# Weight chunks at three layer seams split later, GLA's sums moved to VectorE, and norms moved back in differential attention

## The chip, the cores and the metric

The kernel runs on one core of a Trainium2 chip. The metric is device time of one execution in microseconds (us), lower is better. Three runs of the kernel before took 1218.33, 1220.27 and 1220.82, median 1220.27. Engines are named as in the profile: PE is TensorE, DVE VectorE, ACT ScalarE, POOL GpSimd, and SP the queue that loads the weights.

## What is computed

An AdaLN block and then two more layers, on 256 tokens of width 1024, in fp32 (cut to what the change touches):

```python
# first block: SwiGLU, mixer (short convolution and S5 state space), SwiGLU, final norm
mod = silu(cond) @ w_mod + b_mod                # nine shift, scale and gate rows
x = x + 0.5 * g1 * swiglu(modulate(rms_norm(x, ffn1_norm), sh1, sc1), ffn1_w_gate, ffn1_w_up, ffn1_w_down)
x = x + g2 * mixer(modulate(rms_norm(x, mix_norm), sh2, sc2))
x = x + 0.5 * g3 * swiglu(modulate(rms_norm(x, ffn2_norm), sh3, sc3), ffn2_w_gate, ffn2_w_up, ffn2_w_down)
h = rms_norm(x, final_norm)
# layer 0: gated linear attention (GLA, 4 heads) and an MLP
q, k, v, g, z = split(rms_norm(h, a_norm) @ a_w_in)
log_a = log_sigmoid(z @ w_gate_up + b_gate) / 16          # b = cumsum(log_a) in chunks of 64 tokens
o = causal_sum(q_i . k_j * exp(b_i - b_j)) v_j            # by key, inside and across the chunks
h = h + (rms_norm(o, head_gain) * silu(g)) @ a_w_out
h = h + square(relu(rms_norm(h, mlp_norm0) @ mlp_w1_0)) @ mlp_w2_0
# layer 1: differential attention (8 heads, two maps each), and an MLP
k, v = split(rms_norm(h, kv_norm) @ w_kv); k = rms_norm(k); q = rms_norm(rms_norm(h, b_norm) @ w_q) / 8
a = softmax(q0 k0) - lam * softmax(q1 k1)
h = h + (rms_norm(a @ v, head_gain) * (1 - lambda_init)) @ b_w_out
h = h + square(relu(rms_norm(h, mlp_norm1) @ mlp_w1_1)) @ mlp_w2_1
```

## The kernel before

**Weights.** Each product is made in fp32 out of three matmuls: a weight chunk of 1 MB (128 x 2048) is loaded by SP (L156) into one of three `stage` buffers, ScalarE rounds it into `wh` (L185, two halves of 128x1024), VectorE subtracts to make `wl` (L187, two halves), and `mm3` (L262) runs `wh`, `wl` and `wh` once more against the high and low part of the other operand. `schedule()` writes the order of all chunks down. `Stream.prep` splits the next chunks as long as one of four (later five) slots is free, and `load` issues the load of chunk k once chunk k-3 has been split, since it takes over that buffer. `take(name, j, ahead)` first splits up to `ahead` chunks beyond the one it takes, without an argument as many as there are slots; with `ahead=0` nothing beyond it. A place in the order of `schedule()` decides what is loaded behind what; a place of `prep` in the program decides where the split stands in ScalarE's and VectorE's instructions. Each engine runs its instructions in program order.

**Seams.** `ffn()` (L485) runs a feed-forward layer in steps of 256 hidden units: the up (and gate) chunk of a step is taken and multiplied, the activation makes `hidf`, ScalarE and VectorE split it in `hidh` and `hidl`, and the down product of an earlier step runs beside it. The last three down chunks are taken at its end and go, with the products that use them, into a `Tail`. Down products sum to `acc[i][f]`, i the half of the tokens and f the half of the columns. `turn()` (L438) is the seam: the tail's parts for token half 0, `post(0)` (VectorE adds `acc` to the residual `x`, L398 and L399, ScalarE sums squares, L311), the first of the tail's parts for token half 1, a `prep`, `evac(0)` (the norm's root, then PE transposes into `xnT`, L349, split into `hTh` and `hTl`), the late parts, a `prep`, `post(1)`, and then the first chunks of the new layer on token half 0, with `evac(1)` after the second one. At the seam of ffn2 there is a norm more, the block's final one (L983 to L995). A `swap(n)` after a layer's chunks puts the last down chunk behind the first n chunks of the next layer.

**GLA** (L1284) multiplies the gate, then in `featb` the queries and keys feature by feature (a_in 0 to 3); the values and output gates are a_in 4 to 11. The gate's four products (L1336) become the log decay `E` (L1341 to L1345), a scan over the tokens makes `b`. Six levels of pairs (spans of 1 to 32 tokens) each need `level_e` (differences of `b`, two sums, L1363 and L1364), `exp`, `level_x` (four products with q and k, L1374 to L1378) and `level_mm` on PE (L1385). `across_e`, `across_x` and `across` do the pairs of different chunks (L1426 to L1440). The differences run on GpSimd (name `gt`).

**Differential attention** (L1607): `keys`, `queries` and `values` each take a chunk, multiply and (keys, queries) norm it by head with `qk_norm` (L1628 to L1634, root on ScalarE L303); `turn_qk` transposes, `scores` (L1698), the softmax (L1709 to L1721), `turn_a` (transposes `aT`, copied out by ScalarE, L1733), `outputs` (L1743 to L1752). Four groups of heads run staggered.

Of the kernel before, what the change touches and what calls it, by code (L numbers as in the profile page):

```python
# [18 lines left out]
S = 256  # L19
D = 1024  # L20
KD = 8
CW = 256
# [33 lines left out]
def schedule():  # L56
# [36 lines left out]
    def swap(n):  # L93

        behind.append((len(it) + n, it[-1]))
# [8 lines left out]
    ffn("ffn1", MODS_FFN1, 1)  # L104
    swap(2)
    md = [4 * g + c for g in MODS_MIXER for c in range(4)]
# [29 lines left out]
class Stream:  # L136
# [63 lines left out]
    def take(self, name, j=0, ahead=10 ** 9):  # L200
        self.n_take += 1
        self.prep(self.n_take + ahead)
        W, slot = self.ready.pop((name, j))
        self.used.append(slot)
        return W


class Net:
# [277 lines left out]
    def ffn(self, tail, evac, ups, dn, steps, gated, post, side=None, n_first=3):  # L486
# [48 lines left out]
        for s in range(n_first, steps):  # L535
            res = []
            for u in ups:
                ps = self.bank_u("up")
                begins = s == n_first and u == ups[0]
                self.feat(self.take(u, s, 0 if begins else 10 ** 9), self.hT, v3(ps, 2))  # L540
                self.S.free()
                if s == steps - 1 and u == ups[-1]:
                    self.S.locked.discard((dn, steps - 1))
                res.append(ps)
                if begins:
                    for b in range(n_first):
                        first_hid(b)
                    self.S.prep(10 ** 9)
                    acc = self.acc_banks()
# [12 lines left out]
            if side is not None:  # L562
                side(s)
        last = [(hd, self.take(dn, steps - 3 + n)) for n, hd in enumerate(pend)]
        if gated:
# [718 lines left out]
def gla(N, tail, evac, c):  # L1284
    nc, t, t2, take = N.nc, N.t, N.t2, N.take
    ones, misc, ident = c["ones"], c["misc"], N.ident
    vt, gt, act = nc.vector.tensor_tensor, nc.gpsimd.tensor_tensor, nc.scalar.activation
    v = [t([D], "macc", bufs=2) for i in range(2)]
# [26 lines left out]

    wz = [v3(w, KD) for w in take("a_z")]
    zp = N.bank_u("z")[:16, :S]
# [4 lines left out]

    def featb(ch, dst, scale):
        ps = N.bank_u("qk")
        N.feat(take("a_in", ch), N.hT, v3(ps, 2))
        N.S.free()
        act(out=flat(dst), in_=ps, func=AF.Copy, scale=scale)

    qT, kT = t2([4, S], "qT"), t2([4, S], "kT")
    featb(0, qT[:, 0:2, :], 128 ** -0.5)  # L1330
    gp = []
    for h2 in range(2):
        ps = N.bank_a("gate")
        for k in range(2):
            h = 2 * h2 + k
            nc.tensor.matmul(ps[:, S * k:S * k + S], wgu[:16, 128 * h:128 * h + 128], zT[:16, :], start=True, stop=True)  # L1336
        gp.append(ps)
    e1, mn = t2([4, S], "E", bufs=2), t2([4, S], "E", bufs=2)
# [17 lines left out]
    def level_e(li):  # L1356

        s = LEVELS[li]
        nb = 512 // s
        E = Es[li] = t2([4, S], "E", bufs=2)  # L1360
        ev, bv = (flat(z).rearrange("p (n two s) -> p n two s", two=2, s=s) for z in (E, b))
        ref = bv[:, :, 0, s - 1:s].to_broadcast([128, nb, s])
        gt(out=ev[:, :, 1, :], in0=bv[:, :, 1, :], in1=ref, op=SUB)  # L1363
        gt(out=ev[:, :, 0, :], in0=ref, in1=bv[:, :, 0, :], op=SUB)  # L1364

# [50 lines left out]
    def across_e():  # L1416
# [8 lines left out]
        for i in range(2):  # L1425
            gt(out=ec[:, :, 2 * i, :], in0=tot(2 * i), in1=bc[:, :, 2 * i, :], op=SUB)  # L1426
            nc.gpsimd.tensor_copy(out=ec[:, :, 2 * i + 1, :], in_=bc[:, :, 2 * i + 1, :])
        gt(out=e2[:, :, 0, :], in0=ec[:, :, 0, :], in1=tot(1), op=ADD)
        gt(out=e2[:, :, 1, :], in0=tot(1), in1=bc[:, :, 1, :], op=SUB)
        nc.gpsimd.tensor_copy(out=e2[:, :, 2, :], in_=bc[:, :, 2, :])  # L1430
        gt(out=e2[:, :, 3, :], in0=bc[:, :, 3, :], in1=tot(2), op=ADD)
        xa.extend((E, E2))
# [27 lines left out]
    featb(3, kT[:, 2:4, :], 1.0)  # L1460
    W = take("a_in", 7)
    vt(out=kss[:, 2], in0=qf, in1=kf, op=MUL)
    level_x(0)
    level_e(2)
    exp(Es[2])
    level_x(1)
    level_e(3)
# [10 lines left out]

    W = take("a_in", 8)
    level_x(2)  # L1480
    level_e(4)
    exp(Es[4])
    level_x(3)
    level_e(5)
# [3 lines left out]
    level_mm(3)  # L1488
    W = take("a_in", 9)
    level_x(4)  # L1490
    level_x(5)
    across_e()
    for E in xa:
        exp(E)
    gate_chunk(1, W)
    level_mm(4)
# [3 lines left out]
    gate_chunk(2)  # L1500
    across()
    for hd in range(3):
        act(out=sg[hd], in_=sg[hd], func=AF.Silu)
# [28 lines left out]
    for hp in range(2):  # L1532
        for i in range(2):
            av(i, hp)
    for hd in range(3):
        gated(hd)
    nc.scalar.preload_act_table(AF.Silu)
    W = take("a_in", 11)
    ps = N.bank_u("vg")
    for i in range(2):  # L1540
        N.tokm(W, N.hT, i, ps[:, CW * i:CW * i + CW])
    N.S.free()
    act(out=flat(sg[3]), in_=ps, func=AF.Silu)
    c["load"]("m0", t([D], "macc", bufs=2))
# [62 lines left out]
def diff(N, tail, c):  # L1607
# [171 lines left out]
    turn_qk(1)  # L1779
    queries(2)  # L1780
    turn_a(0)
    scores(1, N.bank_a)
    values(1)
    outputs(0)
    keys(3)
    turn_a(1)
    turn_qk(2)
    turn_o(0)
    queries(3)
    outputs(1)  # L1790
    scores(2, N.bank_a)
    values(2)
# [116 lines left out]
```

## Time and profile before

| what | value |
|---|---|
| median of three runs | 1220.27 us |
| profiled execution | 1219.3 us |
| its span (first to last instruction) | 1217.6 us |
| mean granted clock of TensorE | 0.959 of full |
| PE busy | 1135.3 us, 93% of the span |
| DVE busy | 793.7 us, 65% |
| ACT busy | 613.4 us, 50% |
| POOL busy | 236.6 us, 19% |

A busy share is a mean over stages with different limits. A timeline row gives the start, the length, the engine, the line, the output and the inputs, how many instructions it joins, and in brackets the idle time of the engine before it with the instruction that ended it. PEclk is TensorE's granted clock as a share of its full 2.4 GHz; 0.50 is its lower level of 1.2 GHz. A row `wh<-stage` is a cast of a weight chunk, `wl<-stage,wh` its subtraction. The places that the change touches are ffn1 to mixer (241 to 280 us), ffn2 to GLA (560 to 600), GLA (600 to 700), mlp0 to differential attention (875 to 902) and the attention (925 to 1021).

### The profile page before, as it was taken

To read this page: it belongs to the slowest core of one execution; us is meant where nothing else is said; L and a number is where in the kernel's file an instruction comes from. 1 tells how busy PE (TensorE), PEld (TensorE's weight loads), DVE (VectorE), ACT (ScalarE), POOL (GpSimd) and SP (SyncE) were. 2 spreads that over 40 slices of the span, in tenths; PEclk is the share of its full clock that TensorE was granted. 3 is DMA by queue.
4 is the path that set the end of the run, shared out by engine and by line. 5 is a ranking of instruction groups with operands and counts; after the bars stand their busy time and mean duration, and the time that the engine had idled before them with its cause. 6 is when DMAs were issued, how large, how long until landed. Compare 5 with 4: busy or idle time off the path is not lost.

```text
span 1217.6 us, 18757 instructions
## 1 busy us (share of the span) xinstructions
PE 1135.3 (93%) x7780; PEld 1051.7 (86%) x7780; DVE 793.7 (65%) x934; ACT 613.4 (50%) x941; POOL 236.6 (19%) x304
## 2 busy tenths in 40 slices
PE   1698999989789999999798999999999899999998
PEld 1697999979778999998798889999989897999997
DVE  7698797667968785565466665644468776564541
ACT  3444434455084554354364656655446764664541
POOL 8996399400500000000224100000000000000000
PEclk9698999989789999999897999999999899999999
DMA  8588787535243786565043245755625332385540
GB/s 318 225 327 308 249 322 281 202 139 208 88 155 139 260 324 213 189 242 181 30 144 135 90 141 202 251 178 199 205 107 194 118 118 108 124 291 194 183 143 35
DMA packets 33093, 230.13 MB, mean 189 GB/s; under 512 B 3680, under 2 KB 4064, under 8 KB 5872
## 3 DMA queue, kind: packets, MB, share of 16 engines
q1 hardware_dynamic: 31536, 224.05, 51.2%
q10 hardware_dynamic: 1472, 4.88, 1.1%
q8 instruction: 61, 1.00, 0.3%
q14 instruction: 24, 0.20, 0.0%
HBM read 227.87 MB, written 1.05 MB: 188 GB/s over the span
## 4 chain that ended last, share of the span: by engine, by line
PE 66%; DVE 16%; ACT 8%; POOL 4%; issue 3%; DMA 2%; ACTq 0%; DVEq 0%; POOLq 0%
PE acc L262 26%; PE up L262 25%; PE turn L262 7%; DVE wl L187 7%; ACT wh L185 2%; PE kqv L262 2%; DVE macc L855 1%; POOL s_small L626 1%; PE xnT L349 1%; POOL s_small L629 1%; PE lev L1385 1%; DMA stage<-in_ffn_w_up 1%; PE glu L262 1%; ACT s_lag L748 1%; POOL E L1363 1%
## 5 line engine op out<-in xcount | busy, mean ns | idle before, releaser
L187 DVE TENSOR_TENSOR wl<-stage,wh 128x1024 fp32r<-128x1024 f32 x351 | 425.7, 1261 | 131.3 <-ACT wh L185 131.1
L185 ACT CAST wh<-stage 128x1024 fp32r<-128x1024 f32 x351 | 346.8, 1045 | 126.1 <-PE acc L262 31.4
L262 PE MATMUL up<-hTh,wh 128*128 128x256 f32 x1024 | 289.2, 282 | 1.9 <-ACT s_end L729 1.9
L262 PE MATMUL up<-hTl,wh 128*128 128x256 f32 x1024 | 287.8, 281 | 0.0
L262 PE MATMUL up<-hTh,wl 128*128 128x256 f32 x1024 | 287.8, 281 | 0.0
L262 PEld LDWEIGHTS up<-hTh,wh 128*128 128x128 f32 x1024 | 193.9, 189 | 4.4 <-ACT s_end L729 2.3
L262 PEld LDWEIGHTS up<-hTh,wl 128*128 128x128 f32 x1024 | 196.2, 192 | 0.0
L262 PEld LDWEIGHTS up<-hTl,wh 128*128 128x128 f32 x1024 | 193.6, 189 | 1.5 <-issue 0.2
L262 PE MATMUL acc<-wh,hidh 128*128 128x512 f32 x288 | 115.0, 399 | 4.0 <-ACT wh L185 3.7
L262 PE MATMUL acc<-wl,hidh 128*128 128x512 f32 x288 | 114.0, 396 | 0.8 <-DVE wl L187 0.8
L262 PE MATMUL acc<-wh,hidl 128*128 128x512 f32 x288 | 113.9, 395 | 0.3 <-DVE hidl L296 0.3
L262 PE MATMUL turn<-wh,hTh 128*128 128x256 f32 x320 | 91.4, 286 | 6.2 <-ACT hTh L290 6.2
L262 PE MATMUL turn<-wl,hTh 128*128 128x256 f32 x320 | 90.9, 284 | 2.1 <-DVE wl L187 2.1
L262 PE MATMUL acc<-wh,macc 128*128 128x512 f32 x288 | 92.7, 391 | 0.0
L262 PE MATMUL turn<-wh,hTl 128*128 128x256 f32 x320 | 91.0, 285 | 0.2 <-DVE hTl L291 0.2
L855 DVE SCALAR_TENSOR_TENSOR macc<-stage,cact,macc 128x1024 f32<-128x1024 f32 x63 | 86.1, 1367 | 3.1 <-DMA stage<-in_w_mod 1.4
L262 PEld LDWEIGHTS acc<-wh,hidh 128*128 128x128 f32 x288 | 55.1, 191 | 15.5 <-ACT wh L185 4.1
L262 PEld LDWEIGHTS turn<-wh,hTh 128*128 128x128 f32 x320 | 61.3, 192 | 6.8 <-ACT hTh L290 6.5
L262 PEld LDWEIGHTS acc<-wh,hidl 128*128 128x128 f32 x288 | 54.9, 191 | 13.3 <-DVE hidl L296 1.0
L262 PEld LDWEIGHTS acc<-wl,hidh 128*128 128x128 f32 x288 | 55.0, 191 | 12.1 <-DVE wl L187 1.8
L262 PEld LDWEIGHTS turn<-wl,hTh 128*128 128x128 f32 x320 | 61.2, 191 | 3.1 <-DVE wl L187 2.8
L262 PEld LDWEIGHTS acc<-wh,macc 128*128 128x128 f32 x288 | 54.1, 188 | 11.0
(401 smaller groups left out, 2020.0 us busy)
## 6 DMA issues: line engine op xcount, KB each, us to landing
stage<-in_w SPq DMA_DIRECT2D x64, 1024.0 KB, 4.8
stage<-in_w_mod SPq DMA_DIRECT2D x36, 1024.0 KB, 4.9
stage<-in_ffn_w_gate SPq DMA_DIRECT2D x22, 1024.0 KB, 4.8
stage<-in_ffn_w_up SPq DMA_DIRECT2D x22, 1024.0 KB, 5.0
stage<-in_ffn_w_down SPq DMA_DIRECT2D x22, 1024.0 KB, 5.2
stage<-in_a_in SPq DMA_DIRECT2D x12, 1024.0 KB, 4.9
stage<-in_w_in SPq DMA_DIRECT2D x8, 1024.0 KB, 5.0
stage<-in_w_kv SPq DMA_DIRECT2D x8, 1024.0 KB, 4.9
```

The source lines that it names most:

```text
L185: nc.scalar.copy(out=h[:, b:e], in_=st[:, b:e])
L187: nc.vector.tensor_tensor(out=lo[:, b:e], in0=st[:, b:e], in1=h[:, b:e].bitcast(F32), op=SUB)
L262: self.nc.tensor.matmul(out, lhs(l, k), rhs(r, k), start=first and n == 0, stop=last and n == 3 * n_k - 1)
L349: self.nc.tensor.transpose(out, src, self.ident)
L626: g.tensor_tensor(out=o, in0=x, in1=y, op=op)
L629: g.tensor_scalar(out=o, in0=x, scalar1=s1, scalar2=s2, op0=op0, op1=op1)
L748: nc.scalar.copy(out=self.lag[32 * i:32 * i + 32, 4 * b:4 * b + 4, 32 * i:128], in_=ks[:32, :, 0:128 - 32 * i])
L855: nc.vector.scalar_tensor_tensor(out=acc, in0=wv[:, k, :], scalar=cc, in1=acc, op0=MUL, op1=ADD)
L1363: gt(out=ev[:, :, 1, :], in0=bv[:, :, 1, :], in1=ref, op=SUB)
L1385: nc.tensor.matmul(ps[:, 64 * e:64 * e + 64], ks[:, 128 * e:128 * e + 128], qs[:, 64 * e:64 * e + 64], start=True, stop=True)
```

## The change

1. After ffn1 `swap(1)` replaces `swap(2)`: the last chunks are loaded in the order w_in.6, down.10, w_in.7 instead of w_in.6, w_in.7, down.10.
2. `ffn()` takes the last up chunk and the last three down chunks with `ahead=0`, so that the next layer's chunks are split only where a `prep` of `turn()` comes to them. `take` gains a loop that splits until the wanted chunk is there.
3. In GLA `level_e` and `across_e` run on VectorE (17 sums) and ScalarE (3 copies) instead of GpSimd. a_z and a_in.0 are taken with `ahead=0`; the gate products, with a `prep` of all free slots ahead of them, stand between the two halves of the first query chunk. `level_x(1)` and `level_x(3)` come before the next `level_e`, with splits behind them instead of before. Chunk a_in.11 is taken after `across()` and multiplied in two halves, before and after the products `av`.
4. In the attention the norms of queries 2, keys 3 and queries 3 come after the copy of `aT` of groups 0 and 1 and after `outputs(1)`.

```diff
     ffn("ffn1", MODS_FFN1, 1)
-    swap(2)
+    swap(1)
...
         self.prep(self.n_take + ahead)
+        while (name, j) not in self.ready:
+            n = self.n_slot
+            self.prep(n + 1)
+            assert self.n_slot > n, (name, j)
...
-                self.feat(self.take(u, s, 0 if begins else 10 ** 9), self.hT, v3(ps, 2))
+                ends = s == steps - 1 and u == ups[-1]
+                self.feat(self.take(u, s, 0 if begins or ends else 10 ** 9), self.hT, v3(ps, 2))
...
-        last = [(hd, self.take(dn, steps - 3 + n)) for n, hd in enumerate(pend)]
+        last = [(hd, self.take(dn, steps - 3 + n, 0)) for n, hd in enumerate(pend)]
...
-    wz = [v3(w, KD) for w in take("a_z")]
+    wz = [v3(w, KD) for w in take("a_z", 0, 0)]
...
-    def featb(ch, dst, scale):
-        ps = N.bank_u("qk")
-        N.feat(take("a_in", ch), N.hT, v3(ps, 2))
+    def featb(ch, dst, scale, between=None, ahead=10 ** 9):
+        pv = v3(N.bank_u("qk"), 2)
+        wv = [v3(w, KD) for w in take("a_in", ch, ahead)]
+        for k in range(2):
+            cs = slice(128 * k, 128 * k + 128)
+            N.mm3(pv[:, k, :], lambda l, kk: wv[l][:, kk, cs], lambda r, kk: N.hT[r][:, kk, :], KD)
+            if k == 0 and between is not None:
+                between()
...
-    featb(0, qT[:, 0:2, :], 128 ** -0.5)
+    def gates():
+        N.S.prep(10 ** 9)
...
+    featb(0, qT[:, 0:2, :], 128 ** -0.5, gates, 0)
...
-        gt(out=ev[:, :, 1, :], in0=bv[:, :, 1, :], in1=ref, op=SUB)
-        gt(out=ev[:, :, 0, :], in0=ref, in1=bv[:, :, 0, :], op=SUB)
+        vt(out=ev[:, :, 1, :], in0=bv[:, :, 1, :], in1=ref, op=SUB)
+        vt(out=ev[:, :, 0, :], in0=ref, in1=bv[:, :, 0, :], op=SUB)
...
-            gt(out=ec[:, :, 2 * i, :], in0=tot(2 * i), in1=bc[:, :, 2 * i, :], op=SUB)
-            nc.gpsimd.tensor_copy(out=ec[:, :, 2 * i + 1, :], in_=bc[:, :, 2 * i + 1, :])
+            vt(out=ec[:, :, 2 * i, :], in0=tot(2 * i), in1=bc[:, :, 2 * i, :], op=SUB)
+            nc.scalar.copy(out=ec[:, :, 2 * i + 1, :], in_=bc[:, :, 2 * i + 1, :])
...
-    W = take("a_in", 7)
+    W = take("a_in", 7, 0)
     vt(out=kss[:, 2], in0=qf, in1=kf, op=MUL)
     level_x(0)
+    level_x(1)
+    N.S.prep(10 ** 9)
     level_e(2)
     exp(Es[2])
-    level_x(1)
     level_e(3)
...
     across()
+    W = take("a_in", 11)
+    last_gate = N.bank_u("vg")
+    N.tokm(W, N.hT, 0, last_gate[:, :CW])
...
+    N.tokm(W, N.hT, 1, last_gate[:, CW:])
+    N.S.free()
     for hd in range(3):
         gated(hd)
...
-    queries(2)
+    new_norm("qn", 2)
+    ps = chunk("w_q", 2, hq)
     turn_a(0)
+    qk_norm(ps, [flat(nrm["qn", 2])])
...
-    keys(3)
+    new_norm("kn", 3)
+    ps = chunk("w_kv", 3, hkv)
     turn_a(1)
     turn_qk(2)
+    qk_norm(ps, [flat(nrm["kn", 3])])
     turn_o(0)
-    queries(3)
+    new_norm("qn", 3)
+    ps = chunk("w_q", 3, hq)
     outputs(1)
+    qk_norm(ps, [flat(nrm["qn", 3])])
```

The instructions that move, at three places. ScalarE at the seam ffn2 to GLA, from the last activation of ffn2 to the first squares of the norm; the casts of 128x1024 are those of down.10, a_in.0 and a_in.1, that of 128x128 is a_z. Before:

```order
L476 ACTIVATE act<-up 128x512
L290 CAST hidh_5292<-hidf 128x512
L185 CAST wh<-stage 128x1024 x2
L185 CAST wh<-stage 128x128
L185 CAST wh<-stage 128x1024 x4
L566 ACT_TABLE_LOAD
L311 ACTIVATE hm,rs_ss<-x 128x512
L311 ACTIVATE hm,rs_ss<-xn 128x512
L986 ACTIVATE rs_rr<-rs_ss,eps_75 128x1
```
Now:

```order
L480 ACTIVATE act<-up 128x512
L294 CAST hidh_5292<-hidf 128x512
L185 CAST wh<-stage 128x1024 x2
L571 ACT_TABLE_LOAD
L315 ACTIVATE hm,rs_ss<-x 128x512
L315 ACTIVATE hm,rs_ss<-xn 128x512
L991 ACTIVATE rs_rr<-rs_ss,eps_75 128x1
```
The five casts of a_z, a_in.0 and a_in.1 no longer stand ahead of the table load and the squares; those of a_z and a_in.0 come behind the first copies of `turn` and those of a_in.1 with the eight after `turn`.

VectorE at the start of GLA, from the copy of the gate's input to the first products with queries and keys (`wl` rows are subtractions of a_in chunks, the four E rows are the gates). Before:

```order
L187 TENSOR_TENSOR wl<-stage,wh 128x1024 x6
L1321 COPY zT<-z 16x256
L1341 TENSOR_SCALAR E<-gate,pack 128x256 x4
L1345 TENSOR_TENSOR E<-E 128x1024
L1347 SCALAR_TENSOR_TENSOR b<-gate,E 128x1024
L187 TENSOR_TENSOR wl<-stage,wh 128x1024 x8
L1462 TENSOR_TENSOR ks<-qT,kT 128x1024
```
Now:

```order
L1326 COPY zT<-z 16x256
L187 TENSOR_TENSOR wl<-stage,wh 128x1024 x8
L1355 TENSOR_SCALAR E<-gate,pack 128x256 x4
L1359 TENSOR_TENSOR E<-E 128x1024
L1361 SCALAR_TENSOR_TENSOR b<-gate,E 128x1024
L187 TENSOR_TENSOR wl<-stage,wh 128x1024 x4
L1377 TENSOR_TENSOR E<-b 128x512
L1378 TENSOR_TENSOR E<-b 128x512
L1377 TENSOR_TENSOR E<-b 128x256x2
L1378 TENSOR_TENSOR E<-b 128x256x2
L187 TENSOR_TENSOR wl<-stage,wh 128x1024 x2
L1476 TENSOR_TENSOR ks<-qT,kT 128x1024
```
Eight subtractions stand now between `zT` and the gates' first step, and the four sums of `b` (on GpSimd before) stand between two groups of subtractions.

ScalarE at the seam mlp0 to differential attention, around the last activation of mlp0; the casts are, in this order, w2_0.14, w_kv.0, w_q.0, w_kv.1, w2_0.15, where w2_0.15 is the last down chunk. Before:

```order
L185 CAST wh<-stage 128x1024 x4
L479 ACTIVATE act<-up 128x512
L480 ACTIVATE hidf<-act 128x512
L290 CAST macc<-hidf 128x512
L185 CAST wh<-stage 128x1024 x6
L311 ACTIVATE hm,rs_ss<-x 128x512 x2
```
Now:

```order
L185 CAST wh<-stage 128x1024 x2
L483 ACTIVATE act<-up 128x512
L484 ACTIVATE hidf<-act 128x512
L294 CAST macc<-hidf 128x512
L185 CAST wh<-stage 128x1024 x8
L315 ACTIVATE hm,rs_ss<-x 128x512 x2
```
The two casts of w_kv.0 moved from ahead of the last activation to behind it.

## Rows read from the trace of the kernel before

**Rows 1.** The page, parts 1 and 4: busy shares of the engines, and the chain.

```profile
PE 1135.3 (93%) x7780; PEld 1051.7 (86%) x7780; DVE 793.7 (65%) x934; ACT 613.4 (50%) x941; POOL 236.6 (19%) x304
...
PE 66%; DVE 16%; ACT 8%; POOL 4%; issue 3%; DMA 2%; ACTq 0%; DVEq 0%; POOLq 0%
```

**Rows 2.** Windows by stage: us, busy time of each engine, clock, DMA.

```profile
251.50:257.60 6.10, 5.24 (x12) 3.72 (x13) 4.12 (x5) 2.65 (x3) 0.00 (x0) 0.50 0.82 304
...
584.00:589.00 5.00, 4.92 (x16) 4.27 (x17) 2.37 (x4) 1.17 (x2) 0.00 (x0) 0.52 0.00 0
...
640.00:700.00 60.00, 55.24 (x396) 53.02 (x394) 39.79 (x50) 32.41 (x58) 16.48 (x16) 0.89 0.32 113
...
958.30:964.00 5.70, 5.65 (x21) 5.06 (x22) 4.34 (x9) 4.53 (x17) 0.00 (x0) 0.50 0.38 161
...
1013.00:1018.00 5.00, 3.14 (x16) 2.86 (x16) 3.88 (x5) 3.48 (x6) 0.00 (x0) 0.75 0.92 324
```

**Rows 3.** Timeline of PE, seam ffn1 to mixer (start us, us, engine, line).

```profile
251.52 0.80 PE L262 MATMUL acc<-wh,hidh 128*128 128x512 f32 x1 [3.70 <-ACT wh L185]
...
253.16 0.79 PE L262 MATMUL acc<-wl,hidh 128*128 128x512 f32 x1 [0.84 <-DVE wl L187]
...
274.27 1.03 PE L349 MATMUL xnT<-ident,xn 128*128 128x128 f32 x8
```

**Rows 4.** Timeline of ScalarE and VectorE, same seam.

```profile
248.54 3.88 ACT L185 CAST wh<-stage 128x1024 fp32r<-128x1024 f32 x4
...
269.20 0.68 DVE L398 SCALAR_TENSOR_TENSOR act<-acc,gate 128x512 f32<-128x512 f32 x1
```

**Rows 5.** Timeline of ScalarE and VectorE, seam ffn2 to GLA.

```profile
572.83 2.00 ACT L185 CAST wh<-stage 128x1024 fp32r<-128x1024 f32 x2 [4.36 <-DMA stage<-in_a_in]
...
573.91 2.36 DVE L187 TENSOR_TENSOR wl<-stage,wh 128x1024 fp32r<-128x1024 f32 x2 [3.62 <-ACT wh L185]
...
578.25 0.68 DVE L398 SCALAR_TENSOR_TENSOR act<-acc,gate 128x512 f32<-128x512 f32 x1
```

**Rows 6.** Timeline of PE, same seam.

```profile
571.00 0.40 PE L262 MATMUL acc<-wh,hidl 128*128 128x512 f32 x1
...
584.08 1.94 PE L349 MATMUL xnT<-ident,xn 128*128 128x128 f32 x8 [7.14 <-DVE xn L995]
```

**Rows 7.** Timeline of VectorE, GLA.

```profile
619.09 0.48 DVE L1341 TENSOR_SCALAR E<-gate,pack 128x256 f32<-128x256 f32 x1 [1.24 <-PE gate L1336]
...
630.85 7.15 DVE L187 TENSOR_TENSOR wl<-stage,wh 128x1024 fp32r<-128x1024 f32 x4
...
640.96 4.74 DVE L187 TENSOR_TENSOR wl<-stage,wh 128x1024 fp32r<-128x1024 f32 x4 [2.96 <-ACT wh L185]
```

**Rows 8.** Timeline of PE, GLA.

```profile
646.98 3.54 PE L1400 MATMUL diag<-ones,ks 128*128 128x1 f32 x16 [3.52 <-DVE ks L1462]
...
674.42 3.76 PE L1385 MATMUL lev<-hidf,ks 128*128 128x64 f32 x32 [0.60 <-DVE ks L1378]
```

**Rows 9.** Groups of instructions: busy us, mean ns, idle time before.

```profile
L1374 DVE TENSOR_TENSOR hidf<-qT,E 128x512 f32<-128x512 f32 x6 | 4.5, 753 | 0.0
```

**Rows 10.** Timelines and DMA issues (page, part 6), seam mlp0 to attention.

```profile
878.83 0.33 SPq L156 DMA_DIRECT2D stage<-in_w  x1
...
883.91 2.36 DVE L187 TENSOR_TENSOR wl<-stage,wh 128x1024 fp32r<-128x1024 f32 x2 [0.26 <-ACT wh L185]
...
891.08 0.50 PE L262 MATMUL acc<-wl,macc 128*128 128x512 f32 x1 [0.35 <-DVE wl L187]
...
stage<-in_w SPq DMA_DIRECT2D x64, 1024.0 KB, 4.8
```

**Rows 11.** Timelines of ScalarE and PE, differential attention.

```profile
953.56 1.99 ACT L185 CAST wh<-stage 128x1024 fp32r<-128x1024 f32 x2
...
957.83 0.84 ACT L1733 COPY gate<-aT 128x384 f32<-128x384 f32 x2
...
958.35 2.07 PE L1698 MATMUL s<-row,row 64*128 64x256 f32 x4 [3.05 <-ACT gate L1733]
```

More of the change, by code (lines that the diff above doesn't have):

```diff
@@ L1286, in gla @@
     ones, misc, ident = c["ones"], c["misc"], N.ident
-    vt, gt, act = nc.vector.tensor_tensor, nc.gpsimd.tensor_tensor, nc.scalar.activation
+    vt, act = nc.vector.tensor_tensor, nc.scalar.activation
     v = [t([D], "macc", bufs=2) for i in range(2)]
@@ L1321, in gla @@
     nc.vector.tensor_copy(out=zT[:16], in_=zp)
-    def featb(ch, dst, scale):
-        ps = N.bank_u("qk")
-        N.feat(take("a_in", ch), N.hT, v3(ps, 2))
+    def featb(ch, dst, scale, between=None, ahead=10 ** 9):
[6 more added lines that the diff above has]
+                between()
         N.S.free()
-        act(out=flat(dst), in_=ps, func=AF.Copy, scale=scale)
+        act(out=flat(dst), in_=flat(pv), func=AF.Copy, scale=scale)
     qT, kT = t2([4, S], "qT"), t2([4, S], "kT")
-    featb(0, qT[:, 0:2, :], 128 ** -0.5)
     gp = []
[L1332 to L1337, printed above, removed]
+    def gates():
+        N.S.prep(10 ** 9)
+        for h2 in range(2):
+            ps = N.bank_a("gate")
+            for k in range(2):
+                h = 2 * h2 + k
+                nc.tensor.matmul(ps[:, S * k:S * k + S], wgu[:16, 128 * h:128 * h + 128], zT[:16, :], start=True, stop=True)
+            gp.append(ps)
+    featb(0, qT[:, 0:2, :], 128 ** -0.5, gates, 0)
     e1, mn = t2([4, S], "E", bufs=2), t2([4, S], "E", bufs=2)
@@ L1425, in across_e @@
         for i in range(2):
-            gt(out=ec[:, :, 2 * i, :], in0=tot(2 * i), in1=bc[:, :, 2 * i, :], op=SUB)
-            nc.gpsimd.tensor_copy(out=ec[:, :, 2 * i + 1, :], in_=bc[:, :, 2 * i + 1, :])
[L1428 to L1431, printed above, removed]
+            vt(out=ec[:, :, 2 * i, :], in0=tot(2 * i), in1=bc[:, :, 2 * i, :], op=SUB)
+            nc.scalar.copy(out=ec[:, :, 2 * i + 1, :], in_=bc[:, :, 2 * i + 1, :])
+        vt(out=e2[:, :, 0, :], in0=ec[:, :, 0, :], in1=tot(1), op=ADD)
+        vt(out=e2[:, :, 1, :], in0=tot(1), in1=bc[:, :, 1, :], op=SUB)
+        nc.scalar.copy(out=e2[:, :, 2, :], in_=bc[:, :, 2, :])
+        vt(out=e2[:, :, 3, :], in0=bc[:, :, 3, :], in1=tot(2), op=ADD)
         xa.extend((E, E2))
@@ L1477, in gate_chunk @@
         tok_chunk(8 + hd, [sg[hd][:, i, :] for i in range(2)], W)
-    W = take("a_in", 8)
+    W = take("a_in", 8, 0)
     level_x(2)
+    level_x(3)
+    N.S.prep(10 ** 9)
     level_e(4)
     exp(Es[4])
-    level_x(3)
     level_e(5)
@@ L1488, in gla @@
     level_mm(3)
-    W = take("a_in", 9)
+    W = take("a_in", 9, 0)
     level_x(4)
@@ L1494, in gla @@
         exp(E)
+    N.S.prep(10 ** 9)
     gate_chunk(1, W)
@@ L1537, in gla @@
     nc.scalar.preload_act_table(AF.Silu)
[L1538 to L1543, printed above, removed]
+    act(out=flat(sg[3]), in_=last_gate, func=AF.Silu)
     c["load"]("m0", t([D], "macc", bufs=2))
```

## Prediction

> **What bounds the kernel now.** I read first the shares of the span and the chain that ended last, then the windows by stage, then the timelines of the places that the diff touches. TensorE is busy for 93% of the span, and the chain runs over it for 66% [rows 1]. So an edit gains only where TensorE stands still or runs at the lower of its two clock levels because of a wait, and the chain's 16% on VectorE and 8% on ScalarE are the share in which such a wait can be. The windows show both sorts of place [rows 2]: after the idle stretch at the seam ffn1 to mixer TensorE has a granted clock of 0.50 (1.2 GHz) for 251.5 to 257.6; after that at ffn2 to GLA 0.52 for 584 to 589; in the differential attention 0.50 for 958.3 to 964; and with two shorter gaps, 1013 to 1018, a mean of 0.75. So a gap costs twice, its own length and a stretch at half speed behind it. The second GLA window is the one in which TensorE has some play (55.24 busy of 60) and VectorE works 39.79.
>
> In every seam the last down chunk of the old layer, the first chunks of the new one and the new layer's norm compete for ScalarE (cast `wh`) and VectorE (subtraction `wl`), each in program order.
>
> **Seam ffn1 to mixer.** Before, TensorE waits 3.70 until 251.52 for down.10's cast and goes on with its `wl` at 253.16 [rows 3], because ScalarE casts four halves from 248.54, w_in.7's ahead of down.10's [rows 4], and the activation before them stood behind four casts too, of which two now go. With down.10 second instead of third, and that activation two casts earlier, I find the `wl` product at about 250.95: +2.2. But w_in.7 is then split in the middle of the turn: two casts and two subtractions stand ahead of VectorE's first step of the second norm, which was at 269.20 [rows 4]. Two subtractions are 2.36 [rows 10], and I put 0.35 for the cast that the first of them waits for: 2.7. The step comes at 269.20 - 2.2 + 2.7 = 269.7, and some 4.75 later (the length of that chain now) TensorE's transposes can start, at 274.5. They start at 274.27 now, straight behind other work [rows 3]. So the 2.2 is gone and 0.2 with it; w_in.2 is split later, -0.3; and about 2.4 of idle time ends in a stretch at the lower clock, for which I take -1.2 (bounds: 0, and half of the 6.1 in the first window of rows 2). The sum is **-1.7**, between +2.2 (the norm's wait is hidden) and -3.5.
>
> **Seam ffn2 to GLA.** This is the large gain. ScalarE waits 4.36 for the DMA of an a_in chunk that the kernel wants split ahead, casts it from 572.83, and VectorE subtracts it from 573.91 to 576.27. Only then come the norm's steps on the old layer's sums, the last of the first norm's at 578.25 [rows 5]. These sums had been ready long before: the last product of the first token half's second sum begins at 571.00 and takes 0.40 [rows 6]. From the step at 578.25 to TensorE's transposes at 584.08 is 5.83, with TensorE idle for the last 7.14, since 576.94. Without the split the chain starts at 571.40 and the transposes can go at 577.23; I take 577.28. That is +6.8. The stretch at 0.52 behind the gap did in 4.92 what full clock does in 2.6 [rows 2]: +2.2 if the gap of 0.3 that stays leaves the clock up. The second norm's chain is as long as before and has less TensorE time to hide behind; I give back 0.4. The a_z and a_in splits that were made here go into the second half of the turn, which has play on both engines. The sum is **+8.6**, between +6 (the clock falls all the same, and the second norm shows 0.8) and +9.5.
>
> **GLA.** Its level and across sums go from GpSimd to VectorE, 17 of them, and three copies to ScalarE. With a_in.1 split no longer ahead, a_in.7, its third successor, is loaded later, and the eight subtractions ahead of the gates' first step hold that step from 619.09 [rows 7] until about 622.9, so the decay's chain starts 3.8 late. Against this, before, four subtractions beside GpSimd's sums took 7.15, where the next four take 4.74, with VectorE idle for 2.96 between [rows 7]: 5.4 of slack and contention, and a 128x512 operation on two tensors takes VectorE 0.75 on average [rows 9]. Then a_in.11's split no longer stands ahead of the level products. Followed through, TensorE's first big wait, for `ks`, 3.52 until 646.98, ends 0.7 later, and a later one (0.60 at 674.42) goes [rows 8]; what GpSimd's slower sums held up between them, about 0.4, goes too. The gate products between query halves save nothing, since VectorE holds their result. I come to **+0.3**, from -2.5 (the 3.8 comes through but for a little) to +3.5 (the 3.52 wait all but goes).
>
> The Trainium skill (Perfetto Trace Analysis, section "Optimizing Scalar/DVE Operations") speaks against this edit: where VectorE is saturated it may make sense to give work to ScalarE or even GpSimd, and here the work goes the other way; but it adds that GpSimd and VectorE share a read port, so that moving work between the two might not help. The trace shows the sharing (7.15 against 4.74); by the first half of the rule alone this stage would lose, as rival C does.
>
> **Seam mlp0 to differential attention.** Before, w_kv.0 is split ahead, and that frees the buffer for w2_0.15, whose load is issued at 878.83 [rows 10]. Now w_kv.0 is split after the last activation, in the place where w_q.0 is now (883.91 + 2.36 = 886.27 [rows 10]), and only then is w2_0.15 loaded. It lands 4.8 later [rows 10], and a cast (half of 1.99 [rows 11]) and a subtraction later, at 893.3, TensorE can go on with its `wl`, instead of at 891.08 [rows 10]. That is -2.3 with its hand-over, in two gaps, like those of 1013 to 1018 that had a mean clock of 0.75 [rows 2], so I add -2.0 for a stretch of about 4 at half clock. The sum is **-4.3**, from -2.3 (no drop) to -5.
>
> **Differential attention.** ScalarE is free for the copy of `aT` at 953.56 + 1.99 = 955.55, and does it at 957.83, behind a norm's activation and root; TensorE waits 3.05 for it until 958.35 [rows 11]. With the norm moved behind it, 2.3 earlier. What follows is softmax, in which both VectorE (4.34 of 5.7) and ScalarE (4.53) are full [rows 2], and the moved norm's steps are in that chain; the same exchange for the last query puts the norm ahead of a softmax. I keep **+1.0** of it, between 0 and +2.6 (all of it, and 0.3 of the half-clock stretch).
>
> **Sum.** -1.7 + 8.6 + 0.3 - 4.3 + 1.0 = +3.9. The profiled execution took 1219.3 (span 1217.6), 0.97 below the median of 1220.27. 1219.3 - 3.9 = 1215.4; against the median **1216.4**. A measurement of this kernel tells about 0.2% from no change, 2.4, so faster means under 1217.8 and slower over 1222.7.
>
> **Rivals.** (A) The clock stays up at the first and third seam and the splits there hide better: +0.5 and -2.4 instead of -1.7 and -4.3: a gain of 3.9 + 2.2 + 1.9 = 8.0, **1212.3**. For it: gaps in pieces with work between. Against: 1013 to 1018 [rows 2]. Chance 0.23. (B) Both of these seams reach their lower bounds (-3.5, -5), the second gives only its +6, and GLA -0.5; with the attention's +1.0 that is -2.0, **1222.3** at the worst, and some 1220 halfway from the forecast: no change that can be told. Chance 0.18. (C) The slower side: **VectorE becomes what bounds GLA.** It takes 12 sums of 0.75 [rows 9] and five of half the width that I put at 0.45: 11.2. With the 3.8 by which the decay's chain is late that is 15.0; it gets back 2.4 of contention, 2.4 for a_in.11's split and the 2.96 of idle time [rows 7]. Some 7.2 stay on the path if TensorE has no other work to do meanwhile, instead of +0.3: 1216.4 + 7.5 = **1223.9**. It decides from the point at which VectorE's work is later than TensorE's by more than the gaps now seen (3.52 and 0.60 [rows 8]). Against: 39.79 of 60 busy [rows 2]. Chance 0.11. That the change doesn't do what it says can't be seen from the order: the last splits do move.
>
> **How the numbers follow.** My forecast, with each term within half of its bounds, has 0.48, and its own range is 1213.5 to 1218.5. Faster: 0.43 of it and all of A, 0.66. Slower: C and little of B, 0.12. The rest, 0.22, can't be told from no change. The range takes in A's lower side and B's upper one, leaving out half of C and the tail beyond A: 1210 to 1222.5.
>
> **What would show it.** Right: no ScalarE wait for an a_in DMA ahead of the first norm at ffn2 to GLA, transposes within 1 of the early products, full clock behind; a load of w2_0.15 issued after the last activation of mlp0 and gaps of over 2 for its cast and subtraction; second transposes at the mixer's seam that wait for VectorE by about 2.4; `aT` copied straight behind the cast. Wrong: a granted clock at half in the stretch after ffn2; VectorE releasing TensorE's waits all through GLA's levels (C); w2_0.15 in time (A).

## The result and the profile after

The changed kernel takes 1213.98 us (median of five runs, 1208.77 to 1215.21) against 1220.27: a ratio of 0.994 with a 95% interval of 0.9916 to 0.9964. It is 6.3 us faster where 3.9 had been forecast, and within the range. Its profiled execution, at 1208.77 (span 1206.7), is the fastest of the five, so it shows more of a gain (10.9 in the span) than the medians do; why the runs differ by 6 is part of what follows.

The page of the changed kernel, parts 1 and 4, stands against [rows 1]:

```profile
PE 1129.3 (94%) x7780; PEld 1046.4 (87%) x7780; DVE 797.0 (66%) x951; ACT 614.0 (51%) x944; POOL 212.8 (18%) x284
...
PE 70%; DVE 14%; ACT 8%; POOL 3%; DMA 3%; issue 2%; ACTq 0%; DVEq 0%; POOLq 0%
```

GpSimd's busy time falls from 236.6 to 212.8, VectorE's rises by 3.3 only, and the chain has 14% on VectorE instead of 16%. The sum says little; the stages do. Here the program is cut where TensorE comes to the same work in each kernel: seam 1 with the mixer (ffn1's tenth product to ffn2's first sum), seam 2 (to GLA's first gate input product), GLA (to its second output transposes), seam 3 (mlp0's last sums to the transposes of the attention's norm), and the attention with its output (to mlp1's norm). The lengths are differences of starts in the timelines of TensorE, in us.

| kernel | start to ffn1 | seam 1, mixer | seam 2 | GLA | seam 3 | attention |
|---|---|---|---|---|---|---|
| before | 195.5 | 266.8 | 146.6 | 95.7 | 20.3 | 128.9 |
| changed | 195.9 | 265.9 | 138.0 | 95.1 | 24.2 | 123.9 |
| gain | | 1.0 | 8.6 | 0.6 | -3.9 | 5.0 |
| forecast | | -1.7 | 8.6 | 0.3 | -4.3 | 1.0 |

**Seam 2** of the changed kernel, timelines of ScalarE, VectorE and TensorE in turn (start, length, then as before):

```profile
563.80 2.00 ACT L185 CAST wh<-stage 128x1024 fp32r<-128x1024 f32 x2
...
570.84 0.69 DVE L402 SCALAR_TENSOR_TENSOR act<-acc,gate 128x512 f32<-128x512 f32 x1 [0.64 <-PE acc L266]
...
576.69 1.29 PE L353 MATMUL xnT<-ident,xn 128*128 128x128 f32 x8 [0.34 <-DVE xn L1000]
...
587.31 1.29 PE L353 MATMUL xnT<-ident,xn 128*128 128x128 f32 x8 [0.93 <-DVE xn L1000]
```

Against [rows 5, 6]: ScalarE casts only down.10, the norm's last step on the first half stands at 570.84 and is released by TensorE, and the transposes wait 0.34 instead of 7.14. The second transposes wait 0.93. This is the forecast step by step.

**Seam 3**, timelines of SP, ScalarE and TensorE:

```profile
876.55 0.33 SPq L156 DMA_DIRECT2D stage<-in_w  x1
...
881.46 1.99 ACT L185 CAST wh<-stage 128x1024 fp32r<-128x1024 f32 x2 [2.58 <-DMA stage<-in_w]
...
882.55 0.50 PE L266 MATMUL acc<-wh,macc 128*128 128x512 f32 x1 [1.80 <-ACT wh L185]
...
883.81 0.50 PE L266 MATMUL acc<-wl,macc 128*128 128x512 f32 x1 [0.76 <-DVE wl L187]
```

The last activation of mlp0 is at 871.3 here and at 881.0 before; w2_0.15's load is issued 5.3 behind it, where it was 2.2 ahead of it [rows 10]. ScalarE waits 2.58 for it, and TensorE stands still for 1.80 and 0.76.

**GLA**, timelines of VectorE and TensorE:

```profile
613.57 0.48 DVE L1355 TENSOR_SCALAR E<-gate,pack 128x256 f32<-128x256 f32 x1
...
625.32 4.61 DVE L187 TENSOR_TENSOR wl<-stage,wh 128x1024 fp32r<-128x1024 f32 x4
...
629.85 0.69 DVE L1377 TENSOR_TENSOR E<-b 128x512 f32<-128x512 f32 x1
...
637.95 2.29 PE L1414 MATMUL diag<-ones,ks 128*128 128x1 f32 x10 [5.92 <-DVE ks L1476]
```

The gates' first step is 13.8 behind the first gate input product, where it was 10.1 [rows 7]: 3.7 late, as forecast 3.8. The four subtractions that had taken 7.15 take 4.61, and a sum of `b` takes VectorE 0.69. TensorE's wait for `ks` is now 5.92 instead of 3.52, but it comes where TensorE is ahead by more: it ends 38.2 behind the first gate input product, where it ended 38.0 behind it.

**Attention**, timelines of ScalarE and TensorE, and the window behind:

```profile
949.58 0.86 ACT L1750 COPY gate<-aT 128x384 f32<-128x384 f32 x2
...
950.12 1.13 PE L1715 MATMUL s<-row,row 64*128 64x256 f32 x4 [0.69 <-ACT gate L1750]
...
950.20:957.90 7.70, 7.70 (x61) 7.46 (x62) 6.01 (x12) 4.96 (x17) 0.00 (x0) 1.00 0.39 136
```

The copy of `aT` stands straight behind the cast, the wait is 0.69 instead of 3.05 [rows 11], and the clock behind it is 1.00, where it was 0.50 [rows 2].

### The profile page after: what moved, and what is told of

It reads as the page before. It is cut to its first block, busy times and chain, and to the rows that moved or that the text cites. A ratio compares the mean times of both kernels' runs of the same rounds, so it can differ in the third digit from the quotient of the medians.

```text
span 1206.7 us, 18747 instructions
## 1 busy us (share of the span) xinstructions
PE 1129.3 (94%) x7780; PEld 1046.4 (87%) x7780; DVE 797.0 (66%) x951; ACT 614.0 (51%) x944; POOL 212.8 (18%) x284
## 4 chain that ended last, share of the span: by engine, by line
PE 70%; DVE 14%; ACT 8%; POOL 3%; DMA 3%; issue 2%; ACTq 0%; DVEq 0%; POOLq 0%
PE up L266 27%; PE acc L266 26%; PE turn L266 8%; DVE wl L187 6%; ACT wh L185 2%; PE vg L266 2%; PE kqv L266 1%; PE lev L1399 1%; POOL s_small L631 1%; POOL s_small L634 1%; PE xnT L353 1%; DVE macc L860 1%; DMA stage<-in_w_mod 1%; PE glu L266 1%; ACT s_lag L753 1%
## 5 line engine op out<-in xcount | busy, mean ns | idle before, releaser
L266 PEld LDWEIGHTS turn<-wh,hTh 128*128 128x128 f32 x320 | 61.8, 193 | 6.9 <-ACT hTh L294 6.7
```

What stands on the lines that cost most here:

```text
L266: self.nc.tensor.matmul(out, lhs(l, k), rhs(r, k), start=first and n == 0, stop=last and n == 3 * n_k - 1)
```

## The experiments

Each is timed in five rounds beside the kernel before on the same chip. The first four shared their runs of it (median 1218.75), the next four (1219.62) and the last two (1219.66) too; across these groups the ratios are compared, whose intervals are 0.0010 to 0.0021 to either side (1.2 to 2.6 us). A difference between two kernels of this section is therefore uncertain by some 2.4 to 3.1 us: below, 3.8, 5.4 and 4.8 are clear of it, and 0.2, 1.7, 2.3, 2.4 and 2.9 are not; what is said of those edits rests on the stages of the profiles.

**The changed kernel again**, to see what its runs differ by.

> The changed kernel once more. Its first profiled execution took 1208.77 us, but its median is 1213.98 and its runs reach 1215.21. Theory: what differs between runs is whether TensorE's clock falls behind one of the short gaps that are left (1.3 at the seam ffn1 to mixer, 1.8 at mlp0 to attention, 0.7 in the attention), so this profile shows either the same granted clocks and a time near 1209, or a stretch at 0.50 behind one of these gaps and 2 to 5 us more. Rival: the runs differ by waits for DMA; then gaps that a DMA ends differ between the two profiles and the clocks agree.

Measured: 1212.34 (1209.54 to 1216.32), a ratio of 0.9943 (0.9926 to 0.9961). The profiled execution took 1214.01, 5.2 more than the first. At the places that the change touches, the waits of TensorE are the same within 0.3 (but for one of 0.53 at the second outputs, which is not there), and not the clock (timeline of TensorE, then the window behind):

```profile
951.58 2.07 PE L1715 MATMUL s<-row,row 64*128 64x256 f32 x4 [0.69 <-ACT gate L1750]
...
951.60:959.30 7.70, 7.70 (x36) 7.09 (x37) 6.08 (x12) 4.97 (x17) 0.00 (x0) 0.60 0.41 136
```

With the same wait of 0.69 the attention took 127.7 instead of 123.9. The other 1.4 lies ahead of anything the change touches (start to ffn1: 197.3 against 195.9). So the theory holds for most of it: the clock behind a short gap falls in some executions and not in others. Of the nine profiles of kernels with this attention it was 1.00 in that window in six, and the stage took 123.9 to 125.3; in the three where it fell the stage took 126.5 to 128.1. The clock behind the second outputs, some 55 us later, differs in the same way and is part of these times: 1.00 over 6 us in five of the nine profiles and 0.72 in four, in which the rest of the stage is 1.1 to 1.4 longer.

**The attention as before.**

```diff
-    new_norm("qn", 2)
-    ps = chunk("w_q", 2, hq)
+    queries(2)
     turn_a(0)
-    qk_norm(ps, [flat(nrm["qn", 2])])
...
```

> The change with the differential attention of the kernel before. Theory: the moved norms are worth 5.0 us, 2.4 of it the shorter wait for the copied aT and 2.6 the stretch of 5.7 us at half clock behind it that the shorter gap avoids; so this is 5.0 slower than the changed kernel, TensorE waits 3.05 for the copy and the scores and values behind it run at 0.50. Rival, the forecast's term: 1.0 slower, the softmax takes the rest back whatever the clock.

Measured: 1216.17 (1214.22 to 1217.79), ratio 0.9975 (0.9965 to 0.9985): 3.8 slower than the changed kernel beside it. Timeline of TensorE and the window:

```profile
954.49 2.07 PE L1715 MATMUL s<-row,row 64*128 64x256 f32 x4 [3.05 <-ACT gate L1750]
...
952.20:959.90 7.70, 5.41 (x20) 4.82 (x21) 6.11 (x12) 4.96 (x17) 0.00 (x0) 0.50 0.39 136
```

The wait of 3.05 is back, and the clock is 0.50. The stage takes 129.5. So the part is worth 3.8 by the timed runs, nearer to the theory's 5.0 than to the forecast's 1.0. That the rest up to 5.0 is lost in those runs in which the clock falls behind 0.69 too would fit the nine profiles; it isn't shown, since only the profiled runs have windows.

**Seam 3 as before**: the last up and down chunks of mlp0 are taken with splits ahead again.

```diff
-                ends = s == steps - 1 and u == ups[-1]
+                ends = s == steps - 1 and u == ups[-1] and dn != "w2_0"
...
-        last = [(hd, self.take(dn, steps - 3 + n, 0)) for n, hd in enumerate(pend)]
+        last = [(hd, self.take(dn, steps - 3 + n, 10 ** 9 if dn == "w2_0" else 0)) for n, hd in enumerate(pend)]
```

> The change without its edit at the end of mlp0: w_kv.0 is split ahead of the last activation again. Theory: w2_0.15 is then loaded about 2.4 us earlier against the last activation, its wait (1.80 and 0.76) goes, and so does the slower stretch behind it: 3.9 us faster than the changed kernel, as the profile's difference across this seam. Rival: the 3.9 was mostly clock that happened to fall in that run; then 1.5 to 2.4 faster. A second rival: the gap goes elsewhere in the seam and nothing is gained.

Measured: 1210.64 (1209.97 to 1213.11), ratio 0.993 (0.9916 to 0.9944), 1.7 less than the changed kernel beside it, which the intervals can't tell from 0. The profile can: the seam takes 20.3 instead of 24.2, with the old wait on TensorE's timeline,

```profile
882.28 0.50 PE L266 MATMUL acc<-wl,macc 128*128 128x512 f32 x1 [0.35 <-DVE wl L187]
...
947.20:954.90 7.70, 7.70 (x34) 7.11 (x35) 6.07 (x12) 4.96 (x17) 0.00 (x0) 0.56 0.38 136
```

and the attention's clock fell in this execution (0.56, 128.1), which hides the gain in its own time. In seven profiles with the edit the seam took 22.6 to 24.2, in six of them 23.8 or more; in the five without it 20.3. By the profiles the edit costs 3.5 to 3.9 in the six in which the clock falls behind its waits (0.79 over the 8 us from the `wl` product on) and 2.3 in the one in which it stays at 1.00 (22.6, in the kernel with the sums on GpSimd).

**Seam 1 as before.**

```diff
-    swap(1)
+    swap(2)
...
+                ends = s == steps - 1 and u == ups[-1] and dn != "ffn1_w_down"
```

(and the same condition on the last down chunks.)

> The change without its edit at the seam ffn1 to mixer: chunks in the order w_in.6, w_in.7, down.10, and next chunks split ahead at the end of ffn1. Theory by the profile: the edit is worth +0.6 to +0.9 (3.6 gained at the first transposes, of which 2.4 are given back at the second), so this is 0.6 to 0.9 slower than the changed kernel, with TensorE waiting 3.7 for down.10 and at 0.50 until the norm. Rival, the forecast's term: the edit costs 1.7, so this is 1.7 faster.

Measured: 1212.51 (1208.93 to 1215.65), 0.2 from the changed kernel: no difference. The stage took 267.6, in the kernel before 266.8; with the edit it took 265.9 and 266.0 in two profiles and 267.0 to 267.6 in five. The two sorts differ in the clock behind down.10's wait (windows from the `wl` product on, of the changed kernel's first profile and of the one with seam 3 as before):

```profile
251.20:261.20 10.00, 9.83 (x41) 7.68 (x42) 4.89 (x8) 2.49 (x7) 0.00 (x0) 1.00 0.50 202
```

```profile
252.10:262.10 10.00, 10.00 (x40) 7.98 (x39) 3.85 (x8) 1.93 (x6) 0.00 (x0) 0.89 0.46 187
```

What the edit gains at the first norm it gives back for the most part at the second, whose transposes wait 2.24 to 2.44 in all seven; here the changed kernel's three waits:

```profile
249.56 0.49 PE L266 MATMUL acc<-wh,hidh 128*128 128x512 f32 x1 [1.32 <-ACT wh L185]
...
251.20 0.50 PE L266 MATMUL acc<-wl,hidh 128*128 128x512 f32 x1 [1.15 <-DVE wl L187]
...
273.02 1.35 PE L353 MATMUL xnT<-ident,xn 128*128 128x128 f32 x8 [2.24 <-DVE xn L347]
```

**GLA's sums on GpSimd**, in the new order of the program: `gt` again for the 17 sums, and GpSimd for the 3 copies.

> The change with GLA's 17 sums and 3 copies on GpSimd again, in the new order of the program. Theory: GpSimd's sums take 1.5 each where VectorE takes 0.6, the exponentials and, behind them on ScalarE, the cast of a_in.10 and the copy of the keys wait for them, so the wait of TensorE for ks (5.9) grows by about 2 and the next levels come 2 later too: 2 to 4 us slower than the changed kernel, and subtractions beside GpSimd's sums are slower again (7 for four instead of 4.6). Rival: VectorE is what bounds GLA in the changed kernel, and 10 us of work taken off it makes this 2 to 6 faster.

Measured: 1214.95 (1210.79 to 1220.73), ratio 0.9962 (0.9947 to 0.9976); the changed kernel had 0.9943, so 2.3 us slower by the ratios. The stage (GLA) takes 97.7 instead of 95.1. Timelines of VectorE, GpSimd and TensorE:

```profile
626.47 7.14 DVE L187 TENSOR_TENSOR wl<-stage,wh 128x1024 fp32r<-128x1024 f32 x4
...
632.49 2.02 POOL L1378 TENSOR_TENSOR E<-b 128x512 f32<-128x512 f32 x1
...
640.11 2.08 PE L1414 MATMUL diag<-ones,ks 128*128 128x1 f32 x9 [7.04 <-DVE ks L1476]
```

Four subtractions beside GpSimd's sums take 7.14 again, a sum takes 2.02 where VectorE's takes 0.69, and the wait for `ks` is 7.04. The theory holds, the rival falls: taking the sums off VectorE doesn't shorten GLA, since GpSimd takes longer over them and VectorE's subtractions grow by 2.5. (The 2.02 is beside those subtractions; in the kernel before, a sum of the same size at 665.18 took GpSimd 1.07, while VectorE waited for TensorE.)

**The GLA of before**, with the new seams.

> The change with the GLA function of the kernel before (sums on GpSimd, gates behind the first query chunk, its old order of splits); the seams and the attention as changed. Theory: GLA's edits are worth 0.4 by the two profiles, so from the second transposes of the seam to the first output product this takes 0.4 longer, and the time is the changed kernel's within what can be measured. Rival: the gates' first step, 3.9 late in the changed kernel, costs as much as the sums on VectorE gain, and the two differ by 2 or more to one side.

Measured: 1217.68 (1215.07 to 1221.31), ratio 0.9987 (0.9976 to 0.9999). That is 5.4 slower than the changed kernel by the ratios. The theory falls, and of the rival only the size comes true: GLA takes 102.2, 7.0 more than changed and 6.5 more than in the kernel before, but not for the rival's reason. Timeline of TensorE:

```profile
614.20 3.78 PE L1341 MATMUL gate<-zT,hidf 16*128 16x256 f32 x8 [4.35 <-DVE zT L1326]
...
644.46 1.69 PE L1405 MATMUL diag<-ones,ks 128*128 128x1 f32 x14 [1.74 <-DVE ks L1467]
...
670.27 2.00 PE L1390 MATMUL lev<-hidf,ks 128*128 128x64 f32 x14 [1.76 <-DVE ks L1383]
```

In the old order the splits of all free slots stand ahead of the copy of the gate's input `zT`; with the splits that seam 2 has put off there are eight of them behind a_in.0's, TensorE waits 4.35 for `zT`, and later waits (1.74, 1.76) come on top. So by the stages the seam's gain of 8.6 is worth 2.1 without GLA's new order. Which of GLA's edits saves how much of the 7.0 wasn't tried, but for the sums (2.6 above).

**Seam 2 as before**, with the new GLA (the condition of the diffs above, for `ffn2_w_down`).

> The change with the seam ffn2 to GLA as it was: a_z, a_in.0 and a_in.1 are split ahead of the first norm. Theory: ScalarE waits again for a_in.1's load, the first transposes come 6.8 later and the clock is at 0.5 behind the gap, so this is 8.8 slower than the changed kernel, less what GLA gets back because its gates start earlier (up to 3.8): 5 to 9 slower. Rival: the gap's length is paid but no clock, 3 to 6.8 slower.

Measured: 1215.67 (1213.74 to 1218.58), ratio 0.9963 (0.9952 to 0.9974); against the changed kernel's 0.9943 2.4 slower, less than either theory. Timeline of TensorE:

```profile
584.85 1.94 PE L353 MATMUL xnT<-ident,xn 128*128 128x128 f32 x8 [7.11 <-DVE xn L1000]
...
644.54 1.61 PE L1414 MATMUL diag<-ones,ks 128*128 128x1 f32 x13 [2.63 <-DVE ks L1476]
```

The seam takes 146.5, with the wait of 7.11 back, so the 8.6 is there; but GLA takes only 90.4, 4.7 less than with the splits put off. The splits have not gone away: put off, they stand in front of the gates, and more than half of what the seam gains comes back as GLA's later start.

**Both other seams mended.** Seam 3 as before, and at seam 1 w_in.7 is split straight behind down.10.

```diff
+        last = [(hd, self.take(dn, steps - 3 + n, 10 ** 9 if dn == "w2_0" or (dn == "ffn1_w_down" and n == 2) else 0)) for n, hd in enumerate(pend)]
```

> The change with the seam at mlp0 as before and, at ffn1, w_in.7 split straight behind down.10 and ahead of the first norm. Theory: 4.0 from mlp0; at the mixer the first half's sum waits some 1.4 for VectorE, the second (which ends the chain) does not, and the wait of the second transposes (2.2 to 2.4) goes: together 6 faster than the changed kernel, near 1206. Rival: the first norm's chain is late by a whole subtraction pair (2.3) and eats that gain; then 4 faster.

Measured: 1208.35 (1205.13 to 1210.69), ratio 0.9904 (0.9886 to 0.9921): against the changed kernel's 0.9943 4.8 faster, between the two theories. Seam 3 takes 20.3, and the transposes of seam 1's second norm wait no more; but seam 1 with the mixer still takes 265.5, since the mixer behind the norm took 189.7, against 188.5 to 189.2 with the edit as it was. It isn't a rule: with the next kernel it took 188.8, and the whole stage 263.2, and with the last one 189.8 and 265.4. The windows show what differs, some 90 us behind those transposes (this kernel, then the next one):

```profile
363.40:368.40 5.00, 5.00 (x25) 5.00 (x25) 5.00 (x6) 2.25 (x4) 0.00 (x0) 0.50 0.85 308
```

```profile
360.80:365.80 5.00, 5.00 (x34) 5.00 (x34) 5.00 (x7) 2.59 (x5) 0.00 (x0) 0.73 0.74 257
```

It is the clock again, in a place that no edit touches. So up to the second transposes the mended seam takes 74.4 to 75.8 in its three profiles, against 77.1 to 78.6 with the edit as it was and 78.3 to 78.8 without it.

**Keys first.** On top of the last kernel:

```diff
+    featb(3, kT[:, 2:4, :], 1.0, None, 0)
     level_e(0)
     level_e(1)
     exp(Es[0])
     exp(Es[1])
-    featb(3, kT[:, 2:4, :], 1.0)
```

> The kernel with both seams mended, and in GLA the last half of the keys is taken, multiplied and copied ahead of the sums and exponentials of the first two levels, with a_in.10 split later. Theory: TensorE's wait of 6.1 for ks is one of program order: the copy of the keys, ready at 626.4, stands on ScalarE behind the exponentials, which wait for VectorE's sums, and a_in.10's subtraction stands ahead of ks. Both go, the wait falls to about 1.6, and VectorE's idle 2.1 ahead of it goes as well: 2 to 4 us faster than with the seams alone. Rival: VectorE's own work bounds the levels behind it, the gap comes back at level 2 to 5, and less than 1 is gained.

Measured: 1205.21 (1199.64 to 1207.4), ratio 0.988 (0.9861 to 0.9899), 2.9 faster than the kernel it builds on by the ratios, which their intervals can't tell from 0. GLA takes 92.0 instead of 94.4. Timeline of TensorE:

```profile
631.67 2.21 PE L1414 MATMUL diag<-ones,ks 128*128 128x1 f32 x16 [1.81 <-DVE ks L1476]
...
643.22 0.58 PE L266 MATMUL vg<-wh,hTh 128*128 128x256 f32 x1 [2.41 <-DVE AT L1415]
```

The wait for `ks` falls from 6.08 to 1.81, and 2.41 of it turns up behind the first two levels, where VectorE's list is late now. So the theory holds for what is gained, and the rival for what is left.

**One norm of the attention.** As the last kernel, with the norms of keys 3 and queries 3 where they were before.

> As the kernel with the keys first, but in the attention only the norm of queries 2 comes later; those of keys 3 and queries 3 stand as in the kernel before. Theory: the whole gain of that part (3.8 in the timed runs) comes from queries 2 alone, by the wait of 3.05 that becomes 0.69; the other two moves lengthen TensorE's wait behind the second outputs from 1.3 to 2.4: the same time as with all three, or up to 1 faster. Rival: the three moves together are needed, and this is 1 to 3 slower.

Measured: 1205.08 (1201.92 to 1206.14), ratio 0.9873 (0.9857 to 0.989), the same. Timeline of TensorE:

```profile
1000.93 0.63 PE L353 MATMUL oT<-ident,hm 128*128 128x128 f32 x4 [1.26 <-DVE hm L1769]
```

This wait is 1.26 where it is 2.37 to 2.60 with all three norms moved; from the first outputs to mlp1's norm both took 61.8, as the clock behind the second outputs was lower here. For comparison this wait in the kernel before and in the changed one, and the windows behind it, of this kernel and of the changed one:

```profile
1014.41 0.63 PE L349 MATMUL oT<-ident,hm 128*128 128x128 f32 x4 [1.33 <-DVE hm L1752]
```

```profile
1004.88 0.63 PE L353 MATMUL oT<-ident,hm 128*128 128x128 f32 x4 [2.37 <-DVE hm L1769]
```

```profile
1000.90:1006.90 6.00, 5.45 (x24) 4.67 (x25) 4.29 (x6) 2.99 (x6) 0.00 (x0) 0.72 0.93 351
```

```profile
1004.90:1010.90 6.00, 5.44 (x33) 4.31 (x33) 4.39 (x6) 2.94 (x6) 0.00 (x0) 1.00 0.89 339
```

So the norms of keys 3 and queries 3 cost a wait that is 1.1 longer, and in five of nine profiles the clock behind it gives that back. That the whole stage took 127.1 here is the clock behind the 0.69, which was 0.56 in this execution. The timed runs show no gain beyond that of queries 2's norm.

## Why the prediction was right, and where it wasn't

The sign came out as forecast and the time within the range, 2.4 below the forecast in the first runs and 4.1 below it in the repeated ones: the two terms that were wrong both erred to the slow side. Three of the five are as they were worked out: seam 2 +8.6 (forecast +8.6, in each of ten profiles 138.0 against 146.6), seam 3 -3.9 (forecast -4.3: the waits grew by 2.2, from 0.35 to 1.80 and 0.76, where 2.3 was forecast, and the other 1.7 is the slower stretch, where 2.0 was), and GLA +0.6 (forecast +0.3).

**The attention's term was mis-sized**, +1.0 for 3.8 by the timed runs. The step that failed is "I keep +1.0 of it": that softmax, with VectorE and ScalarE both full, takes back more than half of the 2.3. The softmax behind that wait takes none of it back: even where the clock falls, the first outputs' transposes come 2.0 to 2.8 earlier in the stage. The two other norms do take back 1.1, by the longer wait behind the second outputs: in the two profiles with the lowest clock at both places (127.7 and 128.1 against 128.9 and 129.5) no more than 0.8 to 1.8 is left, near the forecast. So the size that was wrong is the clock's: of the stretch at half clock the range gave 0.3, although the part "What bounds the kernel" says that a gap costs twice. The shorter gap of 0.69 kept the clock at 1.00 in six of nine profiles, worth up to 2.6, and behind the second outputs it stayed up in five.

**Seam 1's term has the wrong sign in the first profile** (+1.0 for -1.7) and is about 0 by the timed runs. The step that failed: I charged the half clock behind the new wait of 2.4 (1.2), but did not credit the stretch of 6.1 at 0.50 behind the old wait of 3.70, which is partly or wholly gone (0.88 to 0.90 over 10 us in five profiles, 1.00 in two). That the second transposes would wait for VectorE by about 2.4 was right (2.24 to 2.44).

**GLA's term came out by a sum that hides a part.** "The gate products between query halves save nothing" misses what the old order costs next to seam 2: the gate products in their new place and `zT` ahead of the splits together avoid its wait of 4.35 (the two weren't tried apart). By the stages, alone, with the old seam, GLA's edits are worth 5.2 (95.7 to 90.4), alone seam 2 is worth 2.1 (8.6 - 6.5); together 9.2. I had put the late gates (3.8) into GLA's term, and so the sum of the two was right.

Rival A (the clock stays up at the first and the third seam) comes true by halves: at seam 1 in two profiles of seven, the first among them; at seam 3 in one, which isn't the first (22.6). Its 1212.3 lies near the measured medians, but by the stages it is the attention, not seam 3, that brought the time there. Rival B falls: seam 2 gave its 8.6 in each profile and seam 1 never came near its lower bound. Rival C falls: with the sums on VectorE GLA is 2.6 shorter than with them on GpSimd. The Trainium skill (Perfetto Trace Analysis, section "Optimizing Scalar/DVE Operations") gives the rule both ways; this trace agrees with its second half, that moving work between GpSimd and VectorE might not help: with the sums on GpSimd a sum takes up to 2.12 instead of 0.69, and the subtractions beside it 7.14 instead of 4.61.

What stays open: the stage gains of the profiles add up to more than the medians differ by (0.4 + 8.6 + 0.6 - 3.9 + 4.0 = 9.7, seam 1 and the attention as means over the profiles with and without the edit, against 6.3). Profiled executions here were mostly among the faster of their kernel, and the kernel before was profiled once; the stages of the executions without a profile can't be read. Why the clock falls behind the same gap in some executions stays open too.

The version that is faster than the kernel before and the changed one is the kernel with the keys first, 1205.21 (0.988), or the one with one norm moved, which can't be told from it: seams 1 and 3 mended, seam 2 and GLA's edits kept, queries 2's norm moved.

## What to carry to other kernels

Putting work off at a seam is a loan: ask who stands behind it in program order at the place where it is paid back, and change that order in the same edit, since neither half may be worth much alone. A split that frees a load buffer is worth its time early, even if nobody wants its result yet. When a wait of TensorE shrinks from some 3 us to under 1, count the slower stretch behind it as well, and take several profiles, because the clock does not fall every time.

## What was not expected of the hardware

The same gaps did not always have the same clock behind them: after waits of 0.88 to 1.07 and 0.69 in the attention the granted clock over the next 7.7 us was 1.00 in six profiles and 0.56, 0.60 and 0.78 in three others, from the same instructions. Behind the second outputs the longer wait (2.37 to 2.60) had a clock of 1.00 behind it in five of nine profiles, and the shorter one (1.26 to 1.33) had 0.72 in all three of its. Together the two places move an execution by up to 4 us, more than several of the edits.
